# Order of work at the start and at the hand-over to attention in a two-layer decoder kernel

## The chip, the core and the metric

The kernel runs on one core of a Trainium2 chip. The metric is device time in microseconds (us) of one execution. Five engines work in parallel, each through its own queue in order: TensorE (PE, with its weight loads PEld), VectorE (DVE), ScalarE (ACT), GpSimd (POOL) and SyncE (SP), whose queue here does nothing but issue DMA transfers. An instruction that waits holds up everything behind it on its own engine.

## The reference, cut to what matters

Two decoder layers work on 1040 tokens (16 meta tokens and 1024 inputs) of 1024 channels in fp32.

```python
h = concat([meta, x])                                    # (1, 1040, 1024)
# layer 0
hn = rms_norm(h, mix_norm_g[0])
h = h + pool_mixer(hn, pool_w, pool_scale)               # causal trailing means over 2, 4, 8, 16 tokens, minus the token, times a (256, 256) matrix per group
hn = rms_norm(h, ffn_norm_g[0])
h = h + (silu(hn @ w_gate) * (hn @ w_up)) @ w_down       # D_FF = 2816
# layer 1
hn = rms_norm(h, mix_norm_g[1])
h = h + diff_attention(hn, w_qkv, w_o, ...)              # 8 heads, two score maps each, T5 bias
h = h + swiglu(rms_norm(h, ffn_norm_g[1]), ...)
return rms_norm(h, final_norm_g)[:, 16:]
```

## The kernel before

**Data.** Channels lie on the 128 partitions (8 blocks, k or m = 0 to 7), tokens along the free dimension, in three chunks c = 0, 1, 2 of 348, 348 and 344 tokens. The residual of chunk c is the tile `h{c}_0`. Every fp32 product is made of three matmuls, high times high, low times high and high times low (`mm3`, L170 to L172), so each operand is split into a rounded part `..h` and a remainder `..l`. The high part is a cast on ACT; the low part is a subtraction, on DVE or on POOL (L160 for weights).

**The start.** The pooling mixer begins from the tokens in rows (`xtok`). `tok_load` brings in the tile `tr_c` of a chunk in three parts j of 128, 128 and the remaining rows (chunk 0: 92; chunks 1 and 2 carry 16 tokens of the one before, so 108 and 104). For each part `stat(j)` is a square sum and a root on ACT and a reciprocal on DVE (`tst`, L339 to L341), `hi(j)` the scaled high part `th` (L348 on ACT, L350 on DVE), `lo(j)` the low part `tl` (L354). The pooling itself is a matmul with a banded matrix (`pl<-bt,th` and `pl<-bt,tl`, L367), then come a split (`ph` on ACT, `pl` on DVE L386), the group matrix (`pm`, weights `pw_h` and `pw_l`) and the residual add `h<-pm` (L396). `start` runs chunk 0's mixer and weaves the beginning of chunk 1's into it. The order on PE, ACT, DVE and POOL is that in which the code is written; the string `START` lists its steps (`h0` is `hi(0)` of chunk 1, `m2` and `m3` are group-matrix steps with their residual adds, `o` ends the squares of chunk 0's second norm, whose sums go to `ms_f` on PE and through TENSOR_REDUCE, L244, to the first SwiGLU).

**The hand-over.** Layer 0's SwiGLU works in 11 pairs of channel blocks; the last pair is f = 20, 21. For it `phase_a(f, c)` makes gate and up products on PE, `s` (gate times up, L565, on DVE) and its split `ah` (ACT) and `al` (DVE, L569); `phase_b` makes the down products `y_0_10_c_m` on PE, 6 matmuls each, and `h<-h,y` on DVE (L581). `done(c)` is the norm ahead of attention, called m10, m11, m12 for c = 0, 1, 2: squares on ACT, their sum `acc_m` on POOL (L200), the sum over partitions `ms_m` on PE (L221), root on ACT and reciprocal on DVE (L246), its spread `mr_m` over the partitions on PE (L250) and a copy on ACT (L253); then for each k a product `xt_m` (DVE, L272), the high part `xh_m` (ACT, L273) and the low part `xl_m` (L275; k = 1, 3, 5 on POOL, the others on DVE). `tailhook` loads and splits the first head's three weights w0, w1, w2 (queries, keys, values). The products of attention are `pj_h_i_c` for head h, weight i, chunk c.

Outside the start, a scheduler that simulates the engines decides the order of the instructions on every engine; inside a `manual_schedule` block it keeps the written order on the engines that the block names. `drain(a, b)` takes steps from two generators in turn. PSUM has four single banks (`psb`) and two double ones (`psa`).

Of the kernel before, what the change touches and what calls it, by code (L numbers as in the profile page):

```python
# [16 lines left out]
KT = D // P  # L17
# [5 lines left out]
NH = 8  # L23
# [8 lines left out]
ZPAD = 164  # L32
NWARM = 12
HOLD = 5
START = "s0 s2 m0 s4 t1 m1 h1 g00 q0 s6 l1 t0 q1 g01 m2 h0 m3 o p1 a0 q2 q3 a1 a2 l0 p0 t2 n g10 g11 x h2 r l2 p2"
FINLAG = (0, 14, 7)
LASTPOOL = 3
PAIRS = {1: 0, 3: 2, 5: 4, 7: 6}
# [34 lines left out]
def drain(*gens):  # L73
    gens = list(gens)
    while gens:
        for g in list(gens):
            if next(g, gens) is gens:
                gens.remove(g)
# [16 lines left out]
def seq(*gens):  # L95
    for g in gens:
        yield from g


class Trunk:  # L100
# [220 lines left out]
    def tok_load(self, c, tok, order=(0, 1, 2)):  # L321
        nc, ap = self.nc, self.ap
        lead = HALO if c else 0
        xl, rows = tok
        for j in order:
            r = rows[j]
            t0 = C0[c] - lead + P * j
            nc.sync.dma_start(xl[:r, j, :], ap["xtok"][t0 : t0 + r])
        return xl, rows

# [67 lines left out]
    def start(self, mx, tok, raw_band, pw, pre, nxt, load_rest):  # L398
# [14 lines left out]
        lo(1)  # L413
        stat(0)
        hi(0, nc.vector)
        stat(2)
        lo(0)
        hi(2, nc.scalar)
        lo(2)
        pw = [self.split_w(*x, nc.gpsimd) for x in pw]  # L420
# [125 lines left out]
    def ffn(self, l, xn, rng, done, head=None, hook=None, tailhook=None, nf=2, pre=None, begin=None, cs=range(NCH)):  # L546
# [46 lines left out]
        for j, fs in enumerate(chunks):  # L593
# [6 lines left out]
            if first:  # L600
                with self.tc.manual_schedule(engines=ORD) if begin else nullcontext():
                    if begin:
                        begin()
                        ws = pre["gu"]
                        down.update(pre["d"])
                if True:
                    for n, c in enumerate(cs):
                        main = seq(*[phase_a(f, c, *ws[f], True) for f in fs], phase_b(j, fs, c))
                        if head and n + 1 < NCH:
                            weave(main, head(n + 1))  # L610
                        drain(main)
                if hook:
                    hook()
            elif j == 1:
                self.nd = 0
                tw = self.twist0(xn)
                run = seq(*[phase_a(f, c, *ws[f]) for c in (1, 0, 2) for f in fs])
                while not next(tw):
                    fill(run, 3)
                while not next(tw):  # L620
                    fill(run, 2)
                drain(run)
            elif last:
                drain(self.down0(j - 1, acts), tw)
                for f in fs:
                    load_d(f)
                aa = [seq(*[phase_a(f, c, *ws[f]) for f in fs]) for c in cs]
                drain(seq(aa[0], aa[1], phase_b(j, fs, cs[0])))
                drain(phase_b(j, fs, cs[1], range(HOLD)), done(cs[0]))
                drain(aa[2])  # L630
                drain(phase_b(j, fs, cs[1], range(HOLD, KT)))
                tailhook()
                drain(phase_b(j, fs, cs[2]), done(cs[1]))
                drain(done(cs[2]))
            else:
                sg = {}
                drain(self.gate0(j, xn, sg))
                drain(self.down0(j - 1, acts))
                drain(self.up0(j, xn, sg, acts))
# [246 lines left out]

    def proj_w(self, h, s, wi):
        if wi not in s["w"]:
            s["w"][wi] = self.load_w(self.ap["wqkv"][wi * NH + h], self.wp, f"w{wi}_{h}", "w", self.nc.gpsimd if h or wi == 2 else None, 4)

    def proj_step(self, h, s, xn, step):
        nc, ap = self.nc, self.ap
# [784 lines left out]
    def run(self):  # L1677
# [4 lines left out]
        with ExitStack() as fctx:  # L1682
# [83 lines left out]
                yield from self.norm_gen(xn1, self.hs[c], c, 0, WC[c], "mix1", f"m1{c}", wide=c > 0)  # L1766
                nc.sync.dma_start(hdram[:, :, C0[c] : C0[c] + WC[c]], self.hs[c][:, :, : WC[c]])

            def tailhook():
                for wi in range(3):  # L1770
                    self.proj_w(0, self.pre[0], wi)

            self.ffn(0, xn0, full, done, head, hook, tailhook, pre=pre, begin=begin)
        ox, ws, part = self.attention(xn1, tail)
# [90 lines left out]
```

## Time and profile before

| | us |
|---|---|
| Median of 3 runs | 2117.39 (2114.24 to 2118.95) |
| Profiled execution | 2117.45 |
| Its span, first to last instruction | 2115.6 |
| Time around the span | 1.85 |
| PE busy | 2066.5 (98%) |
| DVE busy | 1331.5 (63%) |
| ACT busy | 876.9 (41%) |
| POOL busy | 533.9 (25%) |

The profile is of one execution, and its times run from the first instruction. PE is busy for 98% of the span, so a time can fall only where PE waits or runs at its lower clock, or where it has less to do. A row of the timeline has its start, its duration, the engine, the line and the tiles that it writes and reads; where the engine was idle before it, the idle time and what ended it stand in brackets. [...]

### The profile page before, as it was taken

The numbers are of one execution on the slowest core, as the hardware profiler recorded it, in microseconds if no ns is written. First come the engines' busy times: TensorE is split into PE (matmuls) and PEld (weight loads), VectorE is DVE, ScalarE is ACT, GpSimd is POOL, SyncE is SP. The second block draws the span as 40 slices with busy tenths as digits, with TensorE's granted clock in tenths as the row PEclk, the third lists the DMA queues.
The fourth block names the chain that finished last, engine by engine and source line by source line (L and its number), as shares of the span: only waits on it lengthen the run. The fifth ranks groups of instructions, "written<-read, shape, count | busy, mean of one in ns | idle before, by whom it ended". The sixth has DMA issues, their size and how long they took to land.

```text
span 2115.6 us, 30641 instructions
## 1 busy us (share of the span) xinstructions
PE 2066.5 (98%) x11966; PEld 1919.9 (91%) x11966; DVE 1331.5 (63%) x2375; ACT 876.9 (41%) x1843; POOL 533.9 (25%) x658
## 2 busy tenths in 40 slices
PE   7999999999999998999999999999999999999997
PEld 7999999999999998999999998877888888888887
DVE  6666555555455557667677767569656666666665
ACT  5643222333233225666666656444323333333224
POOL 4301101111111016444344424121122122221122
PEclk8999999999999999999999999999999999999998
DMA  7101111111110123212111125431211111111112
GB/s 234 40 24 60 41 61 41 60 51 41 50 51 30 41 74 108 59 60 63 43 53 53 61 97 175 144 136 41 75 45 60 60 40 60 60 41 60 45 36 80
DMA packets 52987, 140.34 MB, mean 66 GB/s; under 512 B 5650, under 2 KB 17467, under 8 KB 52843
## 3 DMA queue, kind: packets, MB, share of 16 engines
q1 hardware_dynamic: 52843, 138.39, 19.9%
q8 instruction: 94, 1.54, 0.3%
q14 instruction: 50, 0.41, 0.1%
HBM read 116.20 MB, written 17.90 MB: 63 GB/s over the span
## 4 chain that ended last, share of the span: by engine, by line
PE 87%; DVE 5%; ACT 3%; DMA 3%; issue 1%; POOL 1%; SPq 0%; POOLq 0%; ACTq 0%; DVEq 0%
PE pj L172 4%; PE pj L170 4%; PE pj L171 4%; PE yd L170 4%; PE yd L171 4%; PE yd L172 4%; PE y L170 3%; PE gu L171 3%; PE gu L172 3%; PE y L171 3%; PE y L172 3%; PE gu L170 3%; PE xw_g L172 3%; PE xw_g L171 3%; PE xw_g L170 3%; PE xw_u L170 3%
## 5 line engine op out<-in xcount | busy, mean ns | idle before, releaser
L170 PE MATMUL pj<-xh_m,w_h 128*128 128x348 f32 (+2 forms) x576 | 187.9, 326 | 1.1 <-DVE oo L1098 1.1
L172 PE MATMUL pj<-xh_m,w_l 128*128 128x348 f32 (+2 forms) x576 | 185.3, 322 | 0.0
L171 PE MATMUL pj<-xl_m,w_h 128*128 128x348 f32 (+2 forms) x576 | 184.2, 320 | 0.0
L1505 DVE TENSOR_TENSOR H<-H,yd 128x512 f32<-128x512 f32 (+1 forms) x184 | 120.7, 662 | 87.8 <-PE yd L172 86.6
L827 DVE TENSOR_TENSOR h<-h,y 128x348 f32<-128x348 f32 (+1 forms) x216 | 108.4, 514 | 82.0 <-PE y L172 82.0
L1312 ACT CAST w_u<-raw_u 128x512 fp32r<-128x512 f32 x88 | 53.1, 621 | 231.2 <-PE y L172 115.3
L170 PE MATMUL yd<-ah,d 128*128 128x512 f32 (+1 forms) x368 | 139.7, 383 | 2.4 <-ACT ah L1312 2.4
L171 PE MATMUL yd<-al,d 128*128 128x512 f32 (+1 forms) x368 | 140.4, 382 | 0.5 <-DVE al L1313 0.5
L172 PE MATMUL yd<-ah,d 128*128 128x512 f32 (+1 forms) x368 | 138.7, 381 | 0.0
L170 PE MATMUL y<-ah,d 128*128 128x348 f32 (+1 forms) x432 | 138.2, 320 | 0.0
L171 PE MATMUL y<-al,d 128*128 128x348 f32 (+1 forms) x432 | 138.0, 320 | 0.0
L172 PE MATMUL y<-ah,d 128*128 128x348 f32 (+1 forms) x432 | 135.7, 320 | 0.0
L1313 DVE TENSOR_TENSOR w_g<-raw_g,w_g 128x512 fp32r<-128x512 f32 x88 | 71.9, 823 | 64.2 <-ACT w_g L1312 57.6
L170 PEld LDWEIGHTS pj<-xh_m,w_h 128*128 128x128 f32 x576 | 108.5, 188 | 1.7 <-DVE oo L1098 1.3
L171 PEld LDWEIGHTS pj<-xl_m,w_h 128*128 128x128 f32 x576 | 108.6, 188 | 0.5
L172 PEld LDWEIGHTS pj<-xh_m,w_l 128*128 128x128 f32 x576 | 108.4, 188 | 0.3
L1313 DVE TENSOR_TENSOR d<-raw_d,d 128x512 fp32r<-128x512 f32 x80 | 70.6, 895 | 44.8 <-ACT d L1312 44.8
L1429 POOL TENSOR_TENSOR z<-raw_g 128x512 f32<-128x512 f32 x16 | 25.9, 1622 | 284.5 <-DVE w_u L1313 227.1
L1018 ACT ACTIVATE e<-s,st 128x144 f32<-128x144 f32 (+6 forms) x112 | 78.9, 706 | 39.3 <-DVE e L1028 19.9
L1050 DVE TENSOR_TENSOR atl<-at,ath 116x512 fp32r<-116x512 f32 (+3 forms) x112 | 61.9, 570 | 38.8 <-ACT ath L1049 38.4
L1312 ACT CAST w_g<-raw_g 128x512 fp32r<-128x512 f32 x88 | 54.6, 622 | 74.4 <-PE xw_u L172 35.1
L170 PEld LDWEIGHTS yd<-ah,d 128*128 128x128 f32 x368 | 69.2, 189 | 15.9 <-ACT ah L1312 3.0
(596 smaller groups left out, 6458.5 us busy)
## 6 DMA issues: line engine op xcount, KB each, us to landing
raw_d<-in_down_dram SPq DMA_DIRECT2D x42, 512.0 KB, 4.0
raw_g<-in_gate_dram SPq DMA_DIRECT2D x36, 512.0 KB, 3.7
raw_u<-in_up_dram SPq DMA_DIRECT2D x36, 512.0 KB, 3.8
raw_w<-in_wqkv_dram SPq DMA_DIRECT2D x24, 512.0 KB, 3.3
odram<-oo SPq DMA_DIRECT2D x28, 256.0 KB, 2.0
ox<-odram SPq DMA_DIRECT2D x4, 1536.0 KB, 9.4
qk<-qk SPq DMA_DIRECT2D x16, 260.0 KB, 2.9
raw_woe<-in_wo_dram SPq DMA_DIRECT2D x8, 512.0 KB, 3.5
```

The source lines that it names most:

```text
L170: nc.tensor.matmul(out, wh, xh, start=first, stop=False, skip_group_check=skip)
L171: nc.tensor.matmul(out, wh, xl, start=False, stop=False, skip_group_check=skip)
L172: nc.tensor.matmul(out, wl, xh, start=False, stop=last, skip_group_check=skip)
L827: nc.vector.tensor_tensor(h, h, ps, op=ALU.add)
L1018: nc.scalar.activation(ev, main[m], AF.Exp, bias=nm, accum_out=sm)
L1050: nc.vector.tensor_tensor(al[:rows, b0 : b0 + len(grp), :], pt[:rows, : len(grp), :], hv.bitcast(F32), op=ALU.subtract)
L1312: self.nc.scalar.copy(hi, src)
L1313: (eng or self.nc.vector).tensor_tensor(lo, src, hi.bitcast(F32), op=ALU.subtract)
L1429: G.tensor_tensor(S[o], a, b, op=op)
L1505: self.nc.vector.tensor_tensor(h, h, ps, op=ALU.add)
```

## The change

There are four edits. In the start, chunk 1's step `h0` moves from between `m2` and `m3` to behind `q3`, and chunk 0's `lo(0)` moves ahead of `stat(2)`. `tok_load` rounds the number of rows of a part up to a multiple of 16, so that chunk 0's last part has 96 rows instead of 92 and chunk 1's 112 instead of 108; chunk 2's 104 stays, since the tokens end there. In the last pair of layer 0's SwiGLU, DVE's order is now the written one, with the second half of the pair for chunk 2 (`aa[2]`) woven into the norm of chunk 0; and the weights of the first head are split singly, w1 behind the end of chunk 1's products, w0 and w2 behind the norm of chunk 1. The low part of w2 moves from POOL to DVE.

```diff
@@ -32,7 +32,7 @@
-START = "s0 s2 m0 s4 t1 m1 h1 g00 q0 s6 l1 t0 q1 g01 m2 h0 m3 o p1 a0 q2 q3 a1 a2 l0 p0 t2 n g10 g11 x h2 r l2 p2"
+START = "s0 s2 m0 s4 t1 m1 h1 g00 q0 s6 l1 t0 q1 g01 m2 m3 o p1 a0 q2 q3 h0 a1 a2 l0 p0 t2 n g10 g11 x h2 r l2 p2"
@@ -325,6 +325,7 @@
             r = rows[j]
             t0 = C0[c] - lead + P * j
+            r = min(-(-r // 16) * 16, L - t0)
             nc.sync.dma_start(xl[:r, j, :], ap["xtok"][t0 : t0 + r])
@@ -413,8 +414,8 @@
         hi(0, nc.vector)
+        lo(0)
         stat(2)
-        lo(0)
         hi(2, nc.scalar)
@@ -626,12 +627,13 @@
-                drain(phase_b(j, fs, cs[1], range(HOLD)), done(cs[0]))
-                drain(aa[2])
-                drain(phase_b(j, fs, cs[1], range(HOLD, KT)))
-                tailhook()
-                drain(phase_b(j, fs, cs[2]), done(cs[1]))
-                drain(done(cs[2]))
+                with self.tc.manual_schedule(engines={mybir.EngineType.DVE}):
+                    drain(seq(phase_b(j, fs, cs[1], range(HOLD)), aa[2], phase_b(j, fs, cs[1], range(HOLD, KT))), done(cs[0]))
+                    tailhook(1)
+                    drain(phase_b(j, fs, cs[2]), done(cs[1]))
+                    tailhook(0)
+                    tailhook(2)
+                    drain(done(cs[2]))
@@ -886,7 +888,7 @@
-            s["w"][wi] = self.load_w(self.ap["wqkv"][wi * NH + h], self.wp, f"w{wi}_{h}", "w", self.nc.gpsimd if h or wi == 2 else None, 4)
+            s["w"][wi] = self.load_w(self.ap["wqkv"][wi * NH + h], self.wp, f"w{wi}_{h}", "w", self.nc.gpsimd if h else None, 4)
@@ -1766,9 +1768,8 @@
-            def tailhook():
-                for wi in range(3):
-                    self.proj_w(0, self.pre[0], wi)
+            def tailhook(wi):
+                self.proj_w(0, self.pre[0], wi)
```

**Start, DVE.** These are ten successive instructions of DVE before, around chunk 0's last residual adds (`h0_0<-pm`); `th_1` and `tl_1` belong to chunk 1's tokens.

```order
L354 SCALAR_TENSOR_TENSOR tl_1_137<-tr_1_114,tst_1_1_139,th_1_136 128x1024
L341 RECIPROCAL tst_1_0_138<-tst_1_0_138 128x1
L396 SCALAR_TENSOR_TENSOR h0_0_92<-pm_0_4_358,vec_75,h0_0_92 128x348
L396 SCALAR_TENSOR_TENSOR h0_0_92<-pm_0_5_366,vec_75,h0_0_92 128x348
L350 TENSOR_SCALAR th_1_136<-tr_1_114,tst_1_0_138 128x1024
L396 SCALAR_TENSOR_TENSOR h0_0_92<-pm_0_6_375,vec_75,h0_0_92 128x348
L396 SCALAR_TENSOR_TENSOR h0_0_92<-pm_0_7_383,vec_75,h0_0_92 128x348
L455 TENSOR_TENSOR sq_f00_5_406<-sq_f00_4_404,sq_f00_5_406 128x348
L455 TENSOR_TENSOR sq_f00_7_411<-sq_f00_6_409,sq_f00_7_411 128x348
L354 SCALAR_TENSOR_TENSOR tl_1_137<-tr_1_114,tst_1_0_138,th_1_136 128x1024
```

In the changed kernel this stands there (line numbers are one higher):

```order
L355 SCALAR_TENSOR_TENSOR tl_1_137<-tr_1_114,tst_1_1_139,th_1_136 128x1024
L342 RECIPROCAL tst_1_0_138<-tst_1_0_138 128x1
L397 SCALAR_TENSOR_TENSOR h0_0_92<-pm_0_4_358,vec_75,h0_0_92 128x348
L397 SCALAR_TENSOR_TENSOR h0_0_92<-pm_0_5_366,vec_75,h0_0_92 128x348
L397 SCALAR_TENSOR_TENSOR h0_0_92<-pm_0_6_374,vec_75,h0_0_92 128x348
L397 SCALAR_TENSOR_TENSOR h0_0_92<-pm_0_7_382,vec_75,h0_0_92 128x348
L456 TENSOR_TENSOR sq_f00_5_405<-sq_f00_4_403,sq_f00_5_405 128x348
L456 TENSOR_TENSOR sq_f00_7_410<-sq_f00_6_408,sq_f00_7_410 128x348
L351 TENSOR_SCALAR th_1_136<-tr_1_114,tst_1_0_138 128x1024
L355 SCALAR_TENSOR_TENSOR tl_1_137<-tr_1_114,tst_1_0_138,th_1_136 128x1024
```

The 1024-wide `th_1_136<-tr_1_114,tst_1_0_138` moved from ahead of the residual adds of `pm_0_6` and `pm_0_7` to behind them and behind two additions of squares.

**Hand-over, DVE.** This is DVE's queue before, where layer 0's last pair ends: `s_0_20_2`, `al_0_20_2`, `s_0_21_2` and `al_0_21_2` are chunk 2's inputs of the last down products, `w0_0_l` a low part of the first head's weights.

```order
L565 TENSOR_TENSOR s_0_20_2_7580<-gu_0_20_2_7531,s_0_20_2_7580 128x344
L565 TENSOR_TENSOR s_0_21_2_7636<-gu_0_21_2_7587,s_0_21_2_7636 128x344
L581 TENSOR_TENSOR h0_0_92<-h0_0_92,y_0_10_0_0_7356 128x348
L581 TENSOR_TENSOR h0_0_92<-h0_0_92,y_0_10_0_1_7364 128x348
L1153 MEMSET qzero_7914 128x128
L581 TENSOR_TENSOR h0_0_92<-h0_0_92,y_0_10_0_2_7372 128x348
L160 TENSOR_TENSOR w0_0_l_7670<-raw_w0_0_7667,w0_0_h_7669 128x256 x4
L569 TENSOR_TENSOR al_0_20_2_7584<-s_0_20_2_7580,ah_0_20_2_7583 128x344
L569 TENSOR_TENSOR al_0_21_2_7640<-s_0_21_2_7636,ah_0_21_2_7639 128x344
L581 TENSOR_TENSOR h0_0_92<-h0_0_92,y_0_10_0_3_7380 128x348
L581 TENSOR_TENSOR h0_0_92<-h0_0_92,y_0_10_0_4_7388 128x348
```

Before, the reciprocal of m10 and its first product stand 10 rows below the last row shown. In the changed kernel the four rows of chunk 2 stand inside and behind the norm m10; `s_0_20_2` and `al_0_20_2` follow its second product, and these are the rows from its fifth product on:

```order
L272 SCALAR_TENSOR_TENSOR xt_m10_4_7591<-h0_0_92,vec_75,acc_m10_7430 128x348
L275 TENSOR_TENSOR xl_m10_7542<-xt_m10_4_7591,xh_m10_7541 128x348
L272 SCALAR_TENSOR_TENSOR xt_m10_5_7601<-h0_0_92,vec_75,acc_m10_7430 128x348
L272 SCALAR_TENSOR_TENSOR xt_m10_6_7611<-h0_0_92,vec_75,acc_m10_7430 128x348
L275 TENSOR_TENSOR xl_m10_7542<-xt_m10_6_7611,xh_m10_7541 128x348
L272 SCALAR_TENSOR_TENSOR xt_m10_7_7621<-h0_0_92,vec_75,acc_m10_7430 128x348
L275 TENSOR_TENSOR xl_m10_7542<-xt_m10_7_7621,xh_m10_7541 128x348
L566 TENSOR_TENSOR s_0_21_2_7638<-gu_0_21_2_7564,s_0_21_2_7638 128x344
L1155 MEMSET qzero_7917 128x128
L570 TENSOR_TENSOR al_0_21_2_7642<-s_0_21_2_7638,ah_0_21_2_7641 128x344
L582 TENSOR_TENSOR h1_0_442<-h1_0_442,y_0_10_1_5_7645 128x348
L582 TENSOR_TENSOR h1_0_442<-h1_0_442,y_0_10_1_6_7653 128x348
```

`s_0_21_2` and `al_0_21_2` moved from ahead of chunk 0's residual adds to behind the whole norm of chunk 0, `qzero` with them, and `w0_0_l` left this stretch. Behind these rows DVE now has the third such add, the low part of w1, the eight residual adds of chunk 2, the reciprocal of m11 and its products, and then the low parts of w0 and w2; before, the products of m10 and the residual adds of chunks 1 and 2 alternated.

**Hand-over, PE.** This is PE's queue before, from the end of chunk 0's keys `pj_0_1_0` on; `w1_0` are the weights of the keys, `w0_0` of the queries, `w2_0` of the values.

```order
L170 MATMUL pj_0_1_0_7926<-xh_m10_7496,w1_0_h_7678 128x348
L171 MATMUL pj_0_1_0_7926<-xl_m10_7497,w1_0_h_7678 128x348
L172 MATMUL pj_0_1_0_7926<-xh_m10_7496,w1_0_l_7679 128x348
L170 MATMUL pj_0_0_0_7955<-xh_m10_7496,w0_0_h_7669 128x332
L171 MATMUL pj_0_0_0_7955<-xl_m10_7497,w0_0_h_7669 128x332
L172 MATMUL pj_0_0_0_7955<-xh_m10_7496,w0_0_l_7670 128x332
L170 MATMUL pj_0_0_0_7955<-xh_m10_7496,w0_0_h_7669 128x332
```

Before, all 24 matmuls of `pj_0_0_0` and all 24 of `pj_0_2_0` follow ahead of `pj_0_1_1`, and the spread of m11's root (`msr_m11`, L250) stands within `pj_0_1_0`. In the changed kernel it is this:

```order
L171 MATMUL pj_0_1_0_7929<-xl_m10_7542,w1_0_h_7671 128x348
L172 MATMUL pj_0_1_0_7929<-xh_m10_7541,w1_0_l_7672 128x348
L250 MATMUL msr_m11_7766<-ident_73,st_m11_7767 128x116 x3
L170 MATMUL pj_0_0_0_7958<-xh_m10_7541,w0_0_h_7814 128x332
L171 MATMUL pj_0_0_0_7958<-xl_m10_7542,w0_0_h_7814 128x332
L170 MATMUL pj_0_2_0_7987<-xh_m10_7541,w2_0_h_7823 128x348
L171 MATMUL pj_0_2_0_7987<-xl_m10_7542,w2_0_h_7823 128x348
L221 MATMUL msr_m12_7854<-ones_74,acc_m12_7830 116x1 x2
L221 MATMUL msr_m12_7854<-ones_74,acc_m12_7830 112x1
L170 MATMUL pj_0_1_1_8014<-xh_m11_7777,w1_0_h_7671 128x348
L171 MATMUL pj_0_1_1_8014<-xl_m11_7778,w1_0_h_7671 128x348
```

The spread moved behind `pj_0_1_0`, and `pj_0_1_1`, which needs the norm m11, moved ahead of 44 matmuls of `pj_0_0_0` and `pj_0_2_0`, of which only the first two each are left in front of it.

## Rows read from the trace of the kernel before

**Rows 1.** The page: busy time, share and instructions of each engine.

```profile
PE 2066.5 (98%) x11966; PEld 1919.9 (91%) x11966; DVE 1331.5 (63%) x2375; ACT 876.9 (41%) x1843; POOL 533.9 (25%) x658
```

**Rows 2.** Windows: length, busy PE, PEld, DVE, ACT, POOL (instructions), PEclk, DMA share, GB/s.

```profile
0.00:47.00 47.00, 34.83 (x172) 32.83 (x173) 27.32 (x49) 25.40 (x47) 21.50 (x24) 0.78 0.79 253
...
80.00:780.00 700.00, 698.75 (x4427) 697.31 (x4427) 383.83 (x724) 215.95 (x421) 94.47 (x77) 1.00 0.14 45
780.00:837.00 57.00, 47.61 (x289) 45.86 (x288) 44.34 (x86) 32.04 (x67) 34.65 (x37) 0.94 0.38 131
...
801.00:808.00 7.00, 5.87 (x23) 5.78 (x24) 2.51 (x6) 3.99 (x8) 3.90 (x5) 0.51 0.14 56
```

**Rows 3.** PE's timeline at the start.

```profile
17.50 2.08 PE L367 MATMUL pl<-bt,tl 128*128 128x256 f32 x8 [5.41 <-DVE tl L354]
...
38.41 0.66 PE L367 MATMUL pl<-bt,th 128*128 128x348 f32 x1 [2.50 <-DVE h L396]
```

**Rows 4.** ACT's timeline at the start.

```profile
14.59 1.06 ACT L339 ACTIVATE tl<-tr 92x1024 fp32r<-92x1024 f32 x1 [4.81 <-DMA tr<-in_xtok_dram]
...
16.29 1.15 ACT L348 ACTIVATE th<-tr,tst 92x1024 fp32r<-92x1024 f32 x1 [0.23 <-DVE tst L341]
...
23.24 2.76 ACT L381 ACTIVATE ph<-pl,vec 128x348 fp32r<-128x348 f32 x6 [3.91 <-PE pl L367]
```

**Rows 5.** DVE's timeline at the start.

```profile
10.01 0.75 DVE L350 TENSOR_SCALAR th<-tr,tst 128x1024 fp32r<-128x1024 f32 x1
16.10 0.16 DVE L341 RECIPROCAL tst<-tst 92x1 f32<-92x1 f32 x1 [5.34 <-ACT tst L340]
16.18 2.58 DVE L354 SCALAR_TENSOR_TENSOR tl<-tr,tst,th 128x1024 fp32r<-128x1024 f32 x2
...
35.19 2.68 DVE L350 TENSOR_SCALAR th<-tr,tst 128x1024 fp32r<-128x1024 f32 x1
...
42.69 0.17 DVE L244 TENSOR_REDUCE st_f<-ms_f 116x3 f32<-116x9 f32 x1 [1.43 <-PE ms_f L221]
```

**Rows 6.** DMA issued up to 3.2 us: count, KB each, us to landing.

```profile
tr<-in_xtok_dram SPq DMA_DIRECT2D x2, 512.0 KB, 5.7
tr<-in_xtok_dram SPq DMA_DIRECT2D x1, 368.0 KB
raw_band<-in_band_dram SPq DMA_DIRECT2D x2, 160.0 KB, 4.0
```

**Rows 7.** Windows of the first loads, columns as in Rows 2.

```profile
2.00:8.00 6.00, 4.29 (x23) 4.11 (x21) 1.85 (x7) 1.66 (x5) 2.18 (x7) 1.00 0.88 298
8.00:14.00 6.00, 3.98 (x24) 3.44 (x24) 2.11 (x3) 1.44 (x3) 2.68 (x6) 1.00 1.03 255
```

**Rows 8.** PE's timeline at the hand-over.

```profile
792.28 0.42 PE L170 MATMUL y<-ah,d_h 128*128 128x348 f32 x1 [2.32 <-DVE h L581]
...
801.57 1.32 PE L221 MATMUL ms_m<-ones,acc_m 128*116 128x1 f32 x6 [5.18 <-POOL acc_m L200]
...
819.29 0.32 PE L170 MATMUL pj<-xh_m,w_h 128*128 128x348 f32 x1
...
836.55 0.41 PE L170 MATMUL pj<-xh_m,w_h 128*128 128x348 f32 x1
```

**Rows 9.** DVE's timeline at the hand-over.

```profile
805.66 1.57 DVE L272 SCALAR_TENSOR_TENSOR xt_m<-h,vec,acc_m 128x348 f32<-128x348 f32 x3 [2.26 <-ACT acc_m L253]
...
822.44 2.33 DVE L272 SCALAR_TENSOR_TENSOR xt_m<-h,vec,acc_m 128x348 f32<-128x348 f32 x3 [2.19 <-ACT acc_m L253]
...
831.26 0.95 DVE L275 TENSOR_TENSOR xl_m<-xt_m,xh_m 128x348 fp32r<-128x348 f32 x2
```

**Rows 10.** POOL's timeline, at the start and at the hand-over.

```profile
18.46 4.85 POOL L160 TENSOR_TENSOR pw_l<-raw_pw,pw_h 128x1024 fp32r<-128x1024 f32 x2 [7.62 <-ACT pw_h L156]
...
788.39 3.13 POOL L200 TENSOR_TENSOR acc_m<-acc_m,sq_m 128x348 f32<-128x348 f32 x3
791.48 3.00 POOL L160 TENSOR_TENSOR w_l<-raw_w,w_h 128x256 fp32r<-128x256 f32 x4
```

## The prediction

> **What bounds the kernel now.** I read the page first: PE is busy for 2066.5 of 2115.6 us [rows 1], so 49 us of idle time and the stretches at the lower clock are all that an order can win or lose. Next I cut the span into windows. The reader is to see that two of them hold much of it and that the edits lie in just these: PE is busy for 34.83 of the first 47 us, at a mean clock of 0.78, and for 47.61 of the 57 us around the hand-over, at 0.94 [rows 2]. After that I read each engine's timeline there for what ended PE's waits. In the start they are 5.41 us for the low part `tl` of the tokens, and 2.50 us for residual adds `h` on DVE [rows 3]. In the hand-over they are 2.32 us for `h`, and 5.18 us for POOL's sum `acc_m` [rows 8]; in the 7 us from that wait on, the granted clock is 0.51 [rows 2]. PE's order is nearly the same before and after, so a change on DVE reaches the end only through such waits.
>
> **Start, the loads.** The square of the 92-row part begins at 14.59, after 4.81 us of waiting for its load, so ACT was free at 9.78 [rows 4]. The loads issued up to that one and with it are two of 512 KB, two of 160 KB and one of 368 KB [rows 6], together 1.75 MB. By 8.0 us 298 GB/s for 6 us, 1.79 MB, had moved [rows 7]. [...] If 96 rows spread evenly, the load lands at about 8.0 plus what 384 KB take at 298 GB/s (1.3), 9.3 us, ahead of ACT's 9.78. [...]
>
> **Start, the order.** With the part there at 9.78, root and reciprocal take 1.5 us (14.59 to 16.10 [rows 4, 5]), to 11.3. On DVE the low part of part 0 now stands ahead of that reciprocal: the high part ends at 10.01 + 0.75 = 10.76, the low one takes 1.29 (half of 2.58) to 12.05 [rows 5]. PE's 5.41 us of waiting, which ended at 17.50 [rows 3], so end at 12.05. The reciprocal follows to 12.2, the high part on ACT (1.15 [rows 4]) to 13.4, its low part on DVE to 14.7. That is the last input of the pooling products. `ph` began at 23.24 [rows 4]; it now begins about 0.7 behind that last input, at 15.4, so 7.8 us earlier. Cover for the rest: the casts `pw_h` follow at 13.4, and POOL's two `pw_l` (4.85 together [rows 10]) end at about 19.3; the second is wanted by the fifth product, at some 20, so it is hidden, and it would cost a few tenths if not.
>
> The step `h0` moved away: the `th` that took 2.68 us [rows 5] stood ahead of the two residual adds for which PE waited 2.50 [rows 3]. The wait goes. What is late next is `th` and its `tl`, behind 4 short rows on DVE; the work is the same and PE wants them only after the sums `ms_f`. So TENSOR_REDUCE, at 42.69 [rows 5], moves by up to 7.8 + 2.5 = 10.3. I take **−9.5**, since parts of this may be lost to small waits on DVE and for chunk 1's loads; 112 rows in place of 108 cost or save nothing that I count, as chunk 1's part is not waited for. Bounds: −11 if PE also keeps the full clock longer, and −5.5 if the load lands no earlier: the high part of part 2 then ends at 17.44 [rows 4], which still frees 3.0 us, and the 2.5 stay.
>
> **Hand-over, what is won first.** DVE drops the low parts of w0 and w1 from among the residual adds, and PE's wait of 2.32 for such an add [rows 8] goes with them; PE's first five products of chunk 1 end at about 793.3 instead of 796.4 (801.57 less 5.18). POOL drops w2's low part (3.00) from among its sums [rows 10]; each sum takes some 1.0 (3.13 for three), so `acc_m` of chunk 0 is done at about 792.9, and PE's 5.18 us of waiting to 801.57 [rows 8] vanish. The spread of m10 is done at 795.3, the last three products of chunk 1 at 798.8, the copy on ACT at 796.9.
>
> **Hand-over, the new wait.** PE's next work is `y_0_10_2_*`, and each of these needs `al_0_21_2`. Before, it was ready ahead of DVE's work on m10; now it stands behind all of it. From 796.9 DVE has 8 `xt` and 5 `xl` of about 0.52 (1.57 for three [rows 9]), 6.8 us; two `s` and two `al` of 0.5 and the memset, 2.1; and some five places where an `xl` or `al` waits for ACT's cast made from the row just before it, 0.65 each (a cast of this size takes 0.46, 2.76 for six [rows 4], and two hand-overs between engines), 3.3. Rows beside POOL's `xl` run longer: three `xt` took 2.33 in one group and 1.57 in another [rows 9], and POOL makes three `xl`; I add 2. `al_0_21_2` is ready at 796.9 + 6.8 + 2.1 + 3.3 + 2 = 811.1. [...] PE idles about 12 us, and the trace shows what follows such a wait: clock 0.51 for 7 us [rows 2]. The 48 matmuls take 0.158 each at full clock (698.75 us for 4427 [rows 2]), 7.6, and about 2.8 more for the low clock (half of the 5.87 us that PE was busy in that window), to 821.8, where before they ended at 819.29 [rows 8].
>
> **Hand-over, the second new wait.** `pj_0_1_0` (24 matmuls, 3.8) ends at 825.6. DVE starts m11 only behind chunk 2's last residual add, and PE gives it the spread only behind `pj_0_1_0`. Before, from the copy that ended DVE's wait at 822.44 to the last `xl` at 832.2 was 9.8 us [rows 9], under 48 matmuls that did not need it. Now only four matmuls stand ahead of `pj_0_1_1`. Spread, copy and that chain, with two evictions of keys in it, are 11.5 to 12.5, so `pj_0_1_1` ends at about 839.0, with some 7 us of idle time in pieces. Then come 44 matmuls (7.0), the spread of m12 (0.7) and 1.5 to 2 for the clock: `pj_0_0_1` starts at about 848.5, where it started at 836.55 [rows 8]. That is **+12**. Bounds: +4.5 if `al_0_21_2` is ready at 807.5 (no waits for ACT), 3.6 earlier, and m11's chain and the clock give back as much again; +16 if PE runs at half clock through most of both stretches. The low parts of w0 and w2, now behind m11 on DVE (a weight took POOL 3.00 [rows 10]), are wanted only behind `pj_0_1_1`, whose 24 matmuls and the two chains ahead of them cover the first; if not, they cost 1 to 2 us of the upper bound.
>
> **Sum.** 2117.45 (the profiled execution, 0.06 over the median of 2117.39) − 9.5 + 12 = 2119.95, said as **2120.0**. A difference under 0.2% (4.2 us) is about what a measurement of this kernel can't tell from no change: the three runs differ by 4.7.
>
> **Rivals.**
> *Faster: the hand-over's waits are short.* The casts on ACT run beside DVE's next rows, and `al_0_21_2` comes by 807 or 808. For it: at half of the places the written order puts another row between a product and its low part. Against: one norm alone took 9.8 us from its first product to its last low part [rows 9], and here four more rows stand in it. 2117.45 − 9.5 + 4.5 = 2112.4. It decides below about 809.
> *Slower: the loads land no earlier.* If the fall to 255 GB/s [rows 7] is a matter of the queue and not of row counts, the part still comes at 14.5, and the start gives 5.5: 2117.45 − 5.5 + 12 = 2124.0. Against: nothing else in the list of loads is of an odd size.
> [...] After both idle stretches, PE's 72 + 44 matmuls would run at half clock for some 8 us longer than I counted, which costs 4: 2124. For it: 0.51 for 7 us after a wait of 5.18 [rows 2, 8], and the new waits are longer and come in pieces.
>
> **How the numbers follow.** I give the forecast 0.45, the short waits 0.22, the loads 0.20, the clock 0.13. The forecast's own range is 2115 to 2125. The range goes from 2110 (short waits with a start of −11) to 2128 (loads no earlier with the upper bound of the hand-over). Within 0.2% of before is 2113.2 to 2121.6: most of the forecast's cases and few of the others, 0.42. Faster holds the short waits: 0.22. Slower, 0.36, holds the other two rivals and the upper part of the forecast.
>
> **What would show it.** Right: ACT's square of the third part begins near 9.8 and `ph` near 15.4; no 2.5 us wait ahead of chunk 1's pooling products; PE waits some 12 us for DVE's `al` ahead of `y` of chunk 2, then shows half clock, then waits in pieces ahead of `pj_0_1_1`; `pj` of w0 and chunk 1 starts 3 us later than before when the start's 9.5 are in. Wrong: a square still waiting to 14; a wait for `al` under 8 us; a wait for `w_l` ahead of `pj_0_0_0`.

## The result, and the profile after

The changed kernel takes 2123.22 us (median of 7 runs, 2122.77 to 2123.62) against 2117.37 (7 runs, 2114.24 to 2119.14): a ratio of 1.0029, 95% interval 1.0017 to 1.0041. It is 5.9 us slower; 2120.0 was forecast. The profiled execution took 2122.83, with a span of 2120.9. The medians in this document count every execution, also one each of 3934.15 us (before, beside e1 to e4), 9841.51 (e3_start_lead) and 6307.76 (e12_hand_first_half), and the ratios leave these three out.

The page first: busy time of each engine, to be set beside [rows 1].

```profile
PE 2069.0 (98%) x11966; PEld 1919.7 (91%) x11966; DVE 1334.2 (63%) x2379; ACT 875.9 (41%) x1843; POOL 527.0 (25%) x654
```

It hides the matter: PE is busy 2.5 us longer with the same number of matmuls, which fits more work at the lower clock, and idle for 2.8 us more of a span that is 5.3 longer. The windows show where (columns as in [rows 2]; PEclk is TensorE's granted clock as a share of its full speed).

```profile
0.00:47.00 47.00, 39.39 (x226) 36.66 (x227) 34.91 (x62) 31.41 (x60) 26.16 (x27) 0.93 0.82 285
8.00:14.00 6.00, 4.40 (x30) 3.86 (x29) 3.07 (x5) 3.55 (x7) 2.25 (x7) 1.00 1.02 376
60.00:70.00 10.00, 7.59 (x55) 7.37 (x53) 5.58 (x10) 4.70 (x9) 2.91 (x3) 0.92 0.01 2
70.00:80.00 10.00, 10.00 (x50) 10.00 (x51) 7.92 (x15) 3.83 (x8) 3.33 (x3) 0.74 0.00 0
780.00:837.00 57.00, 43.57 (x230) 39.81 (x229) 36.25 (x72) 26.53 (x56) 25.17 (x27) 0.82 0.30 103
800.00:810.00 10.00, 5.56 (x21) 5.27 (x21) 8.50 (x15) 3.27 (x7) 3.84 (x4) 0.54 0.26 94
820.00:830.00 10.00, 7.66 (x27) 5.78 (x26) 7.62 (x13) 4.42 (x11) 2.79 (x3) 0.64 0.06 20
```

In the first 47 us PE does 226 matmuls where it did 172 [rows 2]: the start is won. From 60 to 80 us, where nothing was edited, PE now waits and then runs at a clock of 0.74. In the 57 us of the hand-over it does 230 matmuls instead of 289, with clocks of 0.54 and 0.64 in the stretches behind its waits.

**The start.** ACT's timeline answers to [rows 4].

```profile
9.34 1.06 ACT L340 ACTIVATE tl<-tr 128x1024 fp32r<-128x1024 f32 x1 [3.14 <-DMA tr<-in_xtok_dram]
...
10.73 1.04 ACT L340 ACTIVATE tl<-tr 92x1024 fp32r<-92x1024 f32 x1
...
16.39 2.76 ACT L382 ACTIVATE ph<-pl,vec 128x348 fp32r<-128x348 f32 x6
...
66.42 0.46 ACT L564 ACTIVATE s<-gu 128x348 f32<-128x348 f32 x1 [1.08 <-PE gu L172]
...
67.96 1.28 ACT L245 ACT_TABLE_LOAD   x1
69.25 0.30 ACT L245 ACTIVATE st_f<-st_f,eps 116x3 f32<-116x3 f32 x1
```

The 92-row square no longer waits for its load: it runs right behind the part before, at 10.73 instead of 14.59, and `ph` follows at 16.39 instead of 23.24. The part before waits for its own load and begins at 9.34, where it began at 8.30. The last three rows are for the give-back. On PE and DVE the same stretch reads so:

```profile
11.95 1.19 PE L368 MATMUL pl<-bt,th 128*128 128x256 f32 x8 [1.56 <-DVE th L351]
...
27.97 0.43 PE L368 MATMUL pl<-bt,th 128*128 128x348 f32 x1 [0.91 <-DVE h L397]
...
69.91 1.60 PE L250 MATMUL mr_f<-ident,st_f 116*128 116x116 f32 x6 [2.41 <-DVE st_f L246]
```

```profile
33.44 0.17 DVE L244 TENSOR_REDUCE st_f<-ms_f 116x3 f32<-116x9 f32 x1
```

The 5.41 and 2.50 us of waiting [rows 3] are gone. The 1.56 for `th` at 11.95 is new, since the part that begins at 9.34 is late; the 0.91 for `h` stood there before as well (0.92, at 34.84). TENSOR_REDUCE comes 9.25 us earlier than in [rows 5]. But at 69.91 PE waits 2.41 us for chunk 1's root `st_f`. These rows of the kernel before, from PE's and ACT's timelines in the same place, tell why.

```profile
76.94 0.93 PE L250 MATMUL mr_f<-ident,st_f 116*128 116x116 f32 x6 [0.21 <-DVE st_f L246]
```

```profile
74.58 1.28 ACT L245 ACT_TABLE_LOAD   x1
76.38 0.30 ACT L245 ACTIVATE st_f<-st_f,eps 116x3 f32<-116x3 f32 x1 [0.51 <-DVE st_f L244]
76.69 1.28 ACT L563 ACT_TABLE_LOAD   x1
77.98 0.46 ACT L563 ACTIVATE s<-gu 128x348 f32<-128x348 f32 x1
```

Before, the root stood ahead of the next SiLU `s`, with its table load done early, and PE waited 0.21; now it stands behind the SiLU. This stretch is placed by the scheduler, and the new start made it decide otherwise. PE waits, and the granted clock is 0.74 over the ten us from 70 on: the matmuls take 0.49 us up to 74.8 and 0.32 again from 75.34.

**The hand-over.** PE's timeline, beside [rows 8]:

```profile
787.77 0.77 PE L221 MATMUL ms_m<-ones,acc_m 128*116 128x1 f32 x6
790.08 0.92 PE L250 MATMUL mr_m<-ident,st_m 116*128 116x116 f32 x6 [1.54 <-DVE st_m L246]
...
804.44 0.65 PE L170 MATMUL y<-ah,d_h 128*128 128x344 f32 x1 [8.24 <-ACT ah L569]
...
814.61 0.32 PE L172 MATMUL y<-ah,d_l 128*128 128x344 f32 x1
...
818.57 0.82 PE L250 MATMUL msr_m<-ident,st_m 116*128 116x116 f32 x6
...
821.40 0.43 PE L170 MATMUL pj<-xh_m,w_h 128*128 128x348 f32 x1 [0.87 <-ACT xh_m L273]
...
823.96 0.66 PE L171 MATMUL pj<-xl_m,w_h 128*128 128x348 f32 x1 [0.35 <-POOL xl_m L275]
824.42 0.49 PE L172 MATMUL pj<-xh_m,w_l 128*128 128x348 f32 x1
...
840.88 0.41 PE L170 MATMUL pj<-xh_m,w_h 128*128 128x348 f32 x1
```

The 5.18 us for `acc_m` and the 2.32 for `h` are gone. In their place PE waits 8.24 us for the last of `ah` and `al` of chunk 2, and the keys of chunk 1 come in pieces from 821.40 on, with matmuls of 0.49 and 0.66 us where 0.32 is usual: the granted clock is 0.50 from 823.9 to 830.1. These are rows of DVE up to the end of that wait, the chain that the prediction summed, and behind them the low part of w1:

```profile
791.53 0.58 DVE L272 SCALAR_TENSOR_TENSOR xt_m<-h,vec,acc_m 128x348 f32<-128x348 f32 x1 [1.50 <-ACT acc_m L253]
792.66 0.52 DVE L275 TENSOR_TENSOR xl_m<-xt_m,xh_m 128x348 fp32r<-128x348 f32 x1 [0.55 <-ACT xh_m L273]
...
798.65 0.85 DVE L275 TENSOR_TENSOR xl_m<-xt_m,xh_m 128x348 fp32r<-128x348 f32 x1 [0.55 <-ACT xh_m L273]
...
804.42 0.52 DVE L570 TENSOR_TENSOR al<-s,ah 128x344 fp32r<-128x344 f32 x1 [0.40 <-ACT ah L569]
...
806.14 3.64 DVE L160 TENSOR_TENSOR w_l<-raw_w,w_h 128x256 fp32r<-128x256 f32 x4
```

### The profile page after: what moved, and what is told of

Read it like the earlier page. It is cut to its first block, busy times and chain, and to the rows that moved or that the text cites. A ratio compares the mean times of both kernels' runs of the same rounds, so it can differ in the third digit from the quotient of the medians.

```text
span 2120.9 us, 30644 instructions
## 1 busy us (share of the span) xinstructions
PE 2069.0 (98%) x11966; PEld 1919.7 (91%) x11966; DVE 1334.2 (63%) x2379; ACT 875.9 (41%) x1843; POOL 527.0 (25%) x654
## 4 chain that ended last, share of the span: by engine, by line
PE 86%; DVE 5%; ACT 3%; DMA 3%; issue 1%; POOL 1%; SPq 0%; POOLq 0%; ACTq 0%; DVEq 0%
PE pj L171 4%; PE pj L172 4%; PE pj L170 4%; PE y L170 4%; PE y L171 4%; PE y L172 4%; PE gu L171 3%; PE yd L170 3%; PE gu L170 3%; PE gu L172 3%; PE yd L171 3%; PE yd L172 3%; PE xw_g L171 3%; PE xw_g L172 3%; PE xw_g L170 3%; PE xw_u L170 3%
```

## The experiments

Two theories stood against each other. One: the start's 9 us are partly lost to the new order on ACT (B in the texts below), and the hand-over costs about 10 (A) because DVE's written order makes PE wait twice, first for `al` and then for m11. The rival for the first half: the start was never worth 9. The rivals for the second: one of the two waits alone is the cost and the other its echo, either the keys of chunk 1 that come in pieces since the weights are late (C, where a letter is used), or `al` behind m10 (D). Diffs are against the kernel before, where nothing else is said.

The table is worked out from DVE's timelines: when five instructions start, in us for the kernel before and as a difference from it for the others. They are TENSOR_REDUCE (L244), the reciprocal `st_f` of chunk 1, a low part `d` shortly ahead of the hand-over, and two reciprocals of layer 1's later norms, `st_f` and `st_fin`.

| kernel | median, ratio [95%] | 42.69 | 76.71 | 754.56 | 1399.45 | 2083.32 |
|---|---|---|---|---|---|---|
| changed | 2123.22, 1.0029 [1.0017, 1.0041] | -9.25 | -7.13 | -5.42 | +5.06 | +5.52 |
| e1_start_only | 2112.11, 0.9977 [0.9968, 0.9985] | -9.42 | -7.30 | -6.49 | -7.07 | -5.46 |
| e3_start_lead | 2110.75, 0.9970 [0.9959, 0.9981] | -9.01 | -7.57 | -7.76 | -7.68 | -7.70 |
| e8_h0_only | 2118.07, 1.0003 [0.9994, 1.0012] | -2.70 | -0.57 | +1.09 | +0.18 | +0.91 |
| e7_load_and_lo | 2110.00, 0.9968 [0.9956, 0.9981] | -7.87 | -7.87 | -8.10 | -7.93 | -7.50 |
| e11_round_only | 2112.73, 0.9980 [0.9972, 0.9989] | -6.44 | -6.44 | -6.59 | -6.44 | -6.40 |
| e2_hand_only | 2125.55, 1.0044 [1.0031, 1.0056] | -2.21 | -2.20 | -2.41 | +8.12 | +8.09 |
| e6_hand_scheduler | 2112.18, 0.9975 [0.9965, 0.9985] | -1.58 | -1.56 | -1.67 | -8.18 | -7.83 |
| e5_hand_al_first | 2123.55, 1.0033 [1.0020, 1.0045] | -1.96 | -1.96 | -2.41 | +5.44 | +5.44 |
| e12_hand_first_half | 2125.47, 1.0036 [1.0024, 1.0049] | -0.77 | -0.74 | -0.93 | +7.33 | +8.24 |
| e4_hand_weights_early | 2139.62, 1.0109 [1.0096, 1.0123] | -0.71 | +1.04 | +0.62 | +22.40 | +21.69 |
| e9_hand_weights_first | 2133.59, 1.0077 [1.0063, 1.0091] | -0.94 | -0.94 | -1.19 | +13.53 | +14.25 |
| e10_load_lo_scheduler | 2107.27, 0.9955 [0.9942, 0.9967] | -7.23 | -7.23 | -7.33 | -10.22 | -9.84 |

The six kernels whose start is that of before show the first column between -0.71 and -2.21: a single profile places the start only to a us or so, and that of before is the latest of its kind (their mean with it is 41.5). The loads make most of this: in the eight profiles with 92 rows the third part's square begins between 13.69 and 14.59, in the six with 96 rows between 9.77 and 11.49. Counted from the first `ph`, which stands behind the loads, the profiles agree better.

**e1_start_only**, the start's edits with the hand-over as it was.

```diff
-START = "... g01 m2 h0 m3 o p1 a0 q2 q3 a1 a2 ..."
+START = "... g01 m2 m3 o p1 a0 q2 q3 h0 a1 a2 ..."
+            r = min(-(-r // 16) * 16, L - t0)
         hi(0, nc.vector)
+        lo(0)
         stat(2)
-        lo(0)
```

> The three edits of the start alone, the hand-over as before. Theory A (the hand-over costs about 10 us and nothing else does): the lead of 9.2 us at the first norm's TENSOR_REDUCE falls to 5.3 us by 120 us as in the changed kernel, and the run ends at about 2112, 5 us below before. Rival (the lead is lost through the hand-over's edit alone, the start keeps its 9.2): about 2108.

It measured 2112.11, 5.3 us faster. The table shows 9.42 won at TENSOR_REDUCE (8.2 against the mean of the old starts), 6.49 ahead of the hand-over and 5.46 left at the end; the wait of 2.41 for chunk 1's root is there too. The start's gain isn't kept in full.

**e2_hand_only**, the other half of the change, with w2's low part on DVE.

```diff
+                with self.tc.manual_schedule(engines={mybir.EngineType.DVE}):
+                    drain(seq(phase_b(j, fs, cs[1], range(HOLD)), aa[2], phase_b(j, fs, cs[1], range(HOLD, KT))), done(cs[0]))
+                    tailhook(1)
+                    drain(phase_b(j, fs, cs[2]), done(cs[1]))
+                    tailhook(0)
+                    tailhook(2)
+                    drain(done(cs[2]))
```

> The hand-over alone, the start as before. Theory A: PE waits 8 us for the low part of chunk 2 and then in pieces ahead of the keys of chunk 1, and the run ends 10 to 11 us above before, about 2128. Rival (the cost comes only because the start shifted the hand-over against its loads): within 3 us of before.

It measured 2125.55, 8.2 us slower where some 10.5 were expected, with the same wait of 8.24 for `ah`. By the medians the two halves sum to +2.9 and the change measured +5.9; by the ratios they give 1.0021, which lies in the change's interval. So the runs do not show that the halves fail to add.

**e3_start_lead**, e1 with one number of `PACE` changed, the lead that chunk 1's mixer has over the first gate products where the two are woven together, so that the root goes back ahead of the SiLU.

```diff
-PACE = {1: (1, 0.75, 1, 1, 0.7), 2: (4, 1, 1, 1.5, 0.7)}
+PACE = {1: (0.5, 0.75, 1, 1, 0.7), 2: (4, 1, 1, 1.5, 0.7)}
```

> The start's three edits, and the lead of chunk 1's mixer over the first gate products shortened from 1 step to 0.5, which puts the root of chunk 1's second norm back ahead of the SiLU of block 1 on ACT, where it stood before; the hand-over as before. Theory B (3 to 4 us of the start's lead are given back because that root now waits behind the SiLU and a table load): the lead stays near 9 us after 120 us, and the run ends at about 2108 to 2109. Rival (given back to the clock or to the loads, whatever ACT's order): about 2112, as with the start alone.

ACT's timeline has the old order, and PE's wait is 0.38 instead of 2.41:

```profile
67.07 1.28 ACT L245 ACT_TABLE_LOAD   x1
68.81 0.30 ACT L245 ACTIVATE st_f<-st_f,eps 116x3 f32<-116x3 f32 x1 [0.45 <-DVE st_f L244]
69.12 1.28 ACT L564 ACT_TABLE_LOAD   x1
70.42 0.46 ACT L564 ACTIVATE s<-gu 128x348 f32<-128x348 f32 x1
```

```profile
69.37 0.92 PE L250 MATMUL mr_f<-ident,st_f 116*128 116x116 f32 x6 [0.38 <-DVE st_f L246]
```

The lead stays at -7.6 to -7.8 from chunk 1's root to the end, where e1 falls to -5.46. In the medians this is 1.4 us, and the two ranges overlap, so the kept lead is read from the traces; 2110.75 lies between the two expectations. The order on ACT is not all of the give-back. From TENSOR_REDUCE to the root's reciprocal it is 34.02 us before, 36.14 in the change and still 35.46 in e3. From the first `ph` to the low part `d` it is 731.3 us before, 732.8 in the change, 731.7 in e1 and 730.0 in e3, of which the moved `h0` had won 2.4 to 2.6 by TENSOR_REDUCE in the last three. So 3.8 are given back in the change, and still 1.25 in e3 with the old order on ACT; what takes these was not tested.

**e8_h0_only**, **e7_load_and_lo** and **e11_round_only** take the start apart: the moved `h0` alone, the other two edits alone, the rounding alone (the diff lines are those of e1).

> The move of h0 alone. The wait of 2.5 us ahead of chunk 1's pooling products goes, and the scheduler's new order on ACT (SiLU of block 1 ahead of chunk 1's root) gives 2.5 to 3 us back: within 1 us of before, 2116.5 to 2118.5. Rival (the move keeps its 2.5): 2115.

> The start's row rounding and lo(0) alone, h0 and the hand-over as before. Nothing but DVE's lo(0) moves in any queue. TENSOR_REDUCE 6.5 to 7 us earlier than before, and all of it kept, since ACT's order around chunk 1's root is that of before: 2110 to 2111. If the lead is lost downstream whatever ACT's order: 2113 or more.

> The rounding of the rows alone; no queue has another order than before. If the load's landing is the whole gain of the start without h0: within 1 us of the run with lo(0), 2109.5 to 2111. If lo(0) ahead of the reciprocal carries part of it: 2112 or more.

The moved `h0` measures 2118.07, no change. Its lead of 2.70 is nearly gone by the root (0.57), and PE's timeline of e8_h0_only has the wait:

```profile
76.46 1.60 PE L250 MATMUL mr_f<-ident,st_f 116*128 116x116 f32 x6 [2.41 <-DVE st_f L246]
```

Without `h0`, e7 and e11 have the root ahead of the SiLU and keep their lead to within 0.6 us up to the last column. So it is the step `h0` that tips the scheduler, and it pays back what it wins. The rounding is worth 6.4 us against the one profile of before, 5.3 against the mean of the old starts and 0.2%, or 4.2 us, by the ratio. Between e11 and e7, which has `lo(0)` earlier as well, lie 1.1 to 1.5 us in the traces and 2.7 in the medians, but 0.9 of it is the landing of the loads (the third part's square begins at 10.69 and 9.77), and the intervals of the two ratios overlap: what `lo(0)` is worth stays open, some 0.5 us by the traces.

**e6_hand_scheduler**, the hand-over with the weights split singly and w2's low part on DVE, but no written order.

```diff
-                tailhook()
+                tailhook(1)
                 drain(phase_b(j, fs, cs[2]), done(cs[1]))
+                tailhook(0)
+                tailhook(2)
                 drain(done(cs[2]))
```

> The change's order of the weights (w1, then w0 and w2 last, w2's low part on DVE) without the written-down order: the scheduler places DVE's rows. Theory D: it puts al ahead of m10 as before, no 8 us wait, and with w2's low part gone from between POOL's sums the wait for acc_m shrinks from 5 to about 1 or 2 us: 2114 to 2117. If the order of the weights and not DVE's written order were the cost: 2122 or more.

It measured 2112.18, 5.4 us faster than before, some 2 below what was expected, and 13.4 faster than e2. Only the written order tells it apart from e2: the block that fixes DVE's order and, within it, the one line that weaves chunk 2's second half into m10. The scheduler sets all three weights' low parts ahead of m10 again, as DVE's timeline shows, and PE's wait for `acc_m`, 5.18 before [rows 8], is 1.57, which fits w2's low part having left POOL's queue:

```profile
783.49 1.43 DVE L160 TENSOR_TENSOR w_l<-raw_w,w_h 128x256 fp32r<-128x256 f32 x4
784.82 0.95 DVE L569 TENSOR_TENSOR al<-s,ah 128x344 fp32r<-128x344 f32 x2
...
786.53 1.44 DVE L160 TENSOR_TENSOR w_l<-raw_w,w_h 128x256 fp32r<-128x256 f32 x4
...
789.58 3.72 DVE L160 TENSOR_TENSOR w_l<-raw_w,w_h 128x256 fp32r<-128x256 f32 x4
```

```profile
794.13 0.77 PE L221 MATMUL ms_m<-ones,acc_m 128*116 128x1 f32 x6 [1.57 <-POOL acc_m L200]
```

So the written order is the cost. Four kernels ask which part of it.

**e5_hand_al_first**: chunk 2's second half ahead of m10 again, the rest written. This diff and the next three are against the changed kernel's block; the start in all four is that of before.

```diff
                 with self.tc.manual_schedule(engines={mybir.EngineType.DVE}):
-                    drain(seq(phase_b(j, fs, cs[1], range(HOLD)), aa[2], phase_b(j, fs, cs[1], range(HOLD, KT))), done(cs[0]))
+                    drain(aa[2])
+                    drain(seq(phase_b(j, fs, cs[1]), phase_b(j, fs, cs[2])), done(cs[0]))
                     tailhook(1)
-                    drain(phase_b(j, fs, cs[2]), done(cs[1]))
+                    drain(done(cs[1]))
```

> The hand-over alone, written down with the inputs of chunk 2 (s and al of blocks 20 and 21) ahead of everything, and the residual adds of chunks 1 and 2 taken in turn with the norm of chunk 0; the weights' low parts stand where the change has them (w1 ahead of m11, w0 and w2 behind it). Theory D (most of the 9 us is the place of al behind m10: all that follows, m11 too, is late by that wait): no wait for al, and the run ends within 2 us of before, 2115 to 2119. Theory C (the cost is the second wait, which the late low parts force): 6 us or more above before.

It measured 2123.55, 6.0 us slower than before, as C had it. The wait for `ah` is gone, and PE's timeline has others in its place:

```profile
810.39 1.31 PE L221 MATMUL msr_m<-ones,acc_m 128*116 128x1 f32 x6 [5.59 <-POOL acc_m L200]
814.58 0.66 PE L172 MATMUL pj<-xh_m,w_l 128*128 128x348 f32 x1 [2.88 <-DVE w_l L160]
...
823.34 0.42 PE L170 MATMUL pj<-xh_m,w_h 128*128 128x348 f32 x1 [1.41 <-ACT xh_m L273]
```

With `al` in time, m12's sum, w1's low part and m11 make PE wait nearly as long: it is idle for 12.4 us from 780 to 840, and for 13.7 in e2. But this order also weaves chunk 2's residual adds into m10, which the change does not, and m12's sum waits for just these. So e5 shows that an early `al` does not mend a written order by itself, and not what late m11 and weights cost in the change's order.

**e12_hand_first_half**: the reverse. The written order ends behind m10; the weights, m11 and m12 go back to the scheduler.

```diff
-                    tailhook(1)
-                    drain(phase_b(j, fs, cs[2]), done(cs[1]))
-                    tailhook(0)
-                    tailhook(2)
-                    drain(done(cs[2]))
+                tailhook(1)
+                drain(phase_b(j, fs, cs[2]), done(cs[1]))
+                tailhook(0)
+                tailhook(2)
+                drain(done(cs[2]))
```

> The start is as before. On VectorE only the first written line stays (chunk 1's residual adds and chunk 2's second half woven into m10); the weights, chunk 2's residual adds and the norms m11 and m12 go back to the scheduler, which puts all three weights' low parts ahead of m10 again and m11 among the residual adds. The wait for al of chunk 2 so stays as in the change, and what is gone is m11 behind everything. If the stretch of chunk 1's keys is what costs (about 8 of the hand-over's 10 us, as the changed kernel's trace has it: chunk 2's down products end only 0.9 us late there), the time is 2113 to 2119 us. The rival: the late al is the cause, and the keys are late because everything behind it is; then the wait of some 8 us stays and the time is 2121 to 2126 us.

It measured 2125.47, 8.2 us slower than before, as the rival had it. Windows and PE's timeline:

```profile
800.00:820.00 20.00, 10.45 (x45) 9.39 (x45) 13.13 (x24) 8.22 (x18) 7.95 (x9) 0.70 0.17 63
820.00:840.00 20.00, 20.00 (x137) 20.00 (x136) 14.13 (x29) 10.76 (x26) 8.92 (x10) 1.00 0.27 94
840.00:860.00 20.00, 20.00 (x130) 19.95 (x129) 10.91 (x20) 9.46 (x19) 10.63 (x18) 1.00 0.20 55
```

```profile
814.27 0.66 PE L170 MATMUL y<-ah,d_h 128*128 128x344 f32 x1 [8.91 <-ACT ah L568]
...
824.07 0.32 PE L172 MATMUL y<-ah,d_l 128*128 128x344 f32 x1
```

From 820 to 860 PE never waits, so m11 is not late; all of the loss lies in the wait of 8.91 and the clock behind it. Chunk 2's last down product ends at 824.07, where the changed kernel has it at 814.61 with 4.5 us more lead: by 5 us the weights behind m10 did pay in the change, as they let m10 begin earlier, and m11 behind everything took it back.

**e4_hand_weights_early** and **e9_hand_weights_first** move the weights within the written order: w0 and w2 ahead of chunk 2's residual adds, and w1 and w0 ahead of the whole block with w2 in the middle.

```diff
                     tailhook(1)
-                    drain(phase_b(j, fs, cs[2]), done(cs[1]))
                     tailhook(0)
                     tailhook(2)
+                    drain(phase_b(j, fs, cs[2]), done(cs[1]))
                     drain(done(cs[2]))
```

And e9:

```diff
+                    tailhook(1)
+                    tailhook(0)
                     drain(seq(phase_b(j, fs, cs[1], range(HOLD)), aa[2], phase_b(j, fs, cs[1], range(HOLD, KT))), done(cs[0]))
-                    tailhook(1)
+                    tailhook(2)
                     drain(phase_b(j, fs, cs[2]), done(cs[1]))
-                    tailhook(0)
-                    tailhook(2)
                     drain(done(cs[2]))
```

> The hand-over alone, with the low parts of w0 and w2 ahead of chunk 2's residual adds instead of behind the norm of chunk 1; all else of the hand-over as in the change. Theory C (most of the cost is the second wait: the keys of chunk 1 ahead of 44 products of chunk 0, because the low parts come last): the wait of 8 us for chunk 2's low part stays, the waits in pieces ahead of the keys of chunk 1 go, and the run ends at 2119 to 2121, 2 to 4 us above before. Rival (the first wait and the clock behind it are the cost): 2125 to 2127.

> The hand-over alone with the change's written order on DVE (al behind m10, m11 behind chunk 2's adds), only that the low parts of w1 and w0 come before chunk 1's residual adds, and w2's before chunk 2's, so that the raw buffers come free early. Theory C (the cost is the wait ahead of chunk 1's keys, forced because the low parts come last): the 8 us wait for al stays, 44 products of chunk 0 fill the time of m11, and the run ends at 2117 to 2120, within 3 us of before. Rival (DVE's order of al and m10 makes the cost): 2123 or more.

They measured 2139.62, slower than anything expected, and 2133.59, on the side of the rival (2123 or more). In e4 DVE waits for a cast of w2 whose load has no buffer until w1's low part is through, with all of chunk 2's residual adds behind it (DVE's, then PE's timeline):

```profile
822.94 1.43 DVE L160 TENSOR_TENSOR w_l<-raw_w,w_h 128x256 fp32r<-128x256 f32 x4 [5.00 <-ACT w_h L156]
```

```profile
811.26 0.66 PE L170 MATMUL y<-ah,d_h 128*128 128x344 f32 x1 [8.26 <-ACT ah L568]
...
824.85 0.65 PE L170 MATMUL y<-ah,d_h 128*128 128x344 f32 x1 [7.13 <-DVE h L581]
```

In e9 the keys wait for nothing, but `ah` takes 8.98, and the first head's scores lose 7.85 us of 20 (12.15 busy from 860 to 880), where PE waits 3.98 for the exponentials `e`. Why these come late there was not taken apart.

**e10_load_lo_scheduler** puts e7 and e6 together.

> The version that the runs point to: row rounding and lo(0), without the move of h0, and the change's order of the weights left to the scheduler. The two gains (7.5 and 5.4 us) lie in different stages and add: 2104 to 2106. If they share a limit further on: 2108 or more.

It measured 2107.27, the fastest kernel here, between the two expectations: 10 us below the kernel before and 16 below the change. The ratios of e7 and e6 give 0.9943 together, just inside its interval, so whether the two gains add in full stays open.

## Where the prediction was right and wrong, step by step

**The load.** Right. It was to land ahead of ACT's 9.78; the square no longer waits, and `ph` begins 6.85 us earlier where 7.8 were taken. The missing us is the part before, whose load came later (9.34 against 8.30); in e7, where that part begins at 8.29, the square runs at 9.77 and `ph` at 15.38, as forecast. That 96 rows spread evenly, from which the landing at 9.3 was worked out, no run shows; what the trace shows is 376 GB/s from 8 to 14 us where 255 had moved [rows 7], and a square that does not wait. The rival "the loads land no earlier" falls with e11: the rounding alone makes the kernel 0.2% faster.

**The start's sum.** -9.5 was taken, -9.25 measured at TENSOR_REDUCE, or some -8.1 against the mean of the old starts (41.5). The moved `h0` won 2.4 of it (19.45 us from the first `ph` to TENSOR_REDUCE before, 17.05 in the change), where 2.5 were forecast. The step that failed lies behind it: the sum carried these 9.5 unchanged to the end. The scheduler behind the start reacts to it: 2.1 us are lost by chunk 1's root, where PE waits 2.41, and -5.42 is left ahead of the hand-over. e8 and e7 show that the moved `h0` brings the new order on ACT, and e3 that this order loses most of the time; 1.25 us are lost in e3 too.

**The hand-over's first part.** Right. The old waits vanish, and `al` is late. The chain from m10's first product to the last `al` was summed to 14.2 us (796.9 to 811.1) and took 13.4 (791.53 to 804.94), with seven waits for casts on ACT, 3.7 together, where some five of 0.65, 3.3, were assumed. POOL cost less than the 2 us added: two `xl` and one `al` on DVE took 0.85, 0.86 and 0.92 in place of 0.52, 1.1 together, beside rows of POOL of 0.92 or 0.93 that had begun some 0.4 before them. The wait was 8.24 and two short ones of 0.77 and 0.54, 9.6 together, where 12 were forecast; a wait under 8 was to show the forecast wrong, so this was close. Chunk 2's down products were to end 2.5 us later than before (821.8; the terms themselves give 821.5); they ended 4.5 earlier (814.61 against 819.13), and 0.9 later once the lead of 5.42 is taken off.

**The second part.** Right in its mechanism: PE gives the spread behind chunk 0's keys, m11 runs bare, and half clock (0.50 from 823.9 to 830.1) stretches chunk 1's keys. The start of `pj_0_0_1` moved from 836.55 to 840.88 [rows 8], so 9.75 later without the lead, against +12. Of this 8.85 are the keys, against 9.5. From the spread to the last `xl` it took 12.1 us (818.57 to 830.64), as forecast (11.5 to 12.5), but PE was idle for only 2.3 us from 820 to 830 where some 7 in pieces were forecast: its slow matmuls fill the rest.

**The sum.** -9.25 and 3.8 given back, +9.75 at the hand-over and 1.2 spread over layer 1 (+4.33 at `pj_0_0_1`, +5.52 at the end): +5.5, which agrees with the 5.4 of the two profiled executions (2122.83 less 2117.45) and the 5.9 of the medians. The forecast's -9.5 + 12 has the hand-over 2.25 too high, and leaves out the give-back and layer 1, 5.0 together. That it came within 3.2 us is in part luck, as the two misses cancel in part. The 1.2 of layer 1 is of the size by which single profiles differ and was not taken apart. Slower, which came, had been given 0.36, and within 0.2% of before 0.42.

**The rivals.** The short waits did not come; `al` would have had to be ready some 3 us earlier. TensorE did not stay at half clock longer than counted after the first wait: the granted clock was 0.54 from 800 to 810 and 0.50 from 804.4 to 809.1, and the matmuls are at 0.32 us again from 809.16. In the keys, 0.64 from 820 to 830 was part of the loss.

**What stays open.** The cost can't be given to one of the two waits. Late `al` with m11 in time costs 13.3 against e6 (e12), and with late m11 and weights beside it 13.4 (e2): the total is the same. What late m11 and weights would cost alone no run shows, since e5's 11.4 holds a wait of its own making. That the two take the same slack, and that the weights behind m10, which ease the first wait, cause part of the second, fits the traces and is not proved.

## What to carry to other kernels

An edit ahead of a scheduled stretch is also an input to its scheduler: look for new orders far behind it, on engines that the edit does not touch, before the gain is carried to the end. An order written out for one engine fixes what that engine does while it waits for others; here every wait for a cast stood in line, and the scheduler's order, with the weights split singly and one subtraction moved to another engine, was 13 us better than the written one. Where two waits may have a common cause, take each away alone and move nothing else with it: one of the two tests here moved a third thing and met a new wait. Where the landing of loads differs from profile to profile, count a gain from a row behind the loads.

## What the runs showed of the hardware

**Rows of a load.** With 92 rows rounded to 96 the same queue moved 376 GB/s from 8 to 14 us where it had moved 255 [rows 7], and a wait of 4.81 us for 368 KB went away for 16 KB more to carry. The DMA share in this window was 1.03 before [rows 7] and is 1.02 now, so it does not tell the two apart. No row shows single DMA engines, and why 96 rows land sooner was not shown.

**DVE beside POOL.** Four subtractions `w_l` of 128x256 took 1.43 us in e6 at 783.49, with POOL idle, and 3.72 at 789.58, beside POOL's sums of `acc_m`, which ran from 786.70 to 794.07 there:

```profile
786.70 7.37 POOL L200 TENSOR_TENSOR acc_m<-acc_m,sq_m 128x348 f32<-128x348 f32 x6
```

That is 0.57 us more for each. In the change the four `w_l` of w1 at 806.14 take 3.64, beside POOL's sums at 806.10 (three in 3.06), and the eight of w0 and w2, with POOL idle, take 2.77 together. But not every row beside POOL is longer: in e6 the group at 786.53 took its usual 1.44 while POOL's six sums ran from 786.70 on. These six took 1.23 us each, where the sums at 798.84 and 799.72 in the kernel before, with DVE idle, took 0.92. Why rows of one engine are longer beside the other was not shown.
